# Seven block products instead of eight in 16 of the 22 column pairs of a feed-forward product

## The chip, the cores and the metric

The kernel runs on one core of a Trainium2 chip. The metric is the device time of one execution in microseconds (us). Every time below is of the kernel before the change.

## The reference

One inference step of a small backbone: two trunk layers over 640 tokens (512 latent tokens and 128 context tokens, which share all weights). Each layer is a token mixer of three kinds and then a gated feed-forward block. Everything is fp32, and what the change touches is the feed-forward block:

```python
D_MODEL = 1024
D_FF = -(-8 * D_MODEL // (3 * 256)) * 256      # 2816 = 22 blocks of 128

h = rmsnorm(x, p['g_pre_ffn']) * (1.0 + sc2) + sh2
ff_a, ff_b = jnp.split(h @ p['w_ffn_in'], 2, axis=-1)      # (640,1024) @ (1024,5632)
x = x + gt2 * rmsnorm((jax.nn.silu(ff_a) * ff_b) @ p['w_ffn_out'], p['g_post_ffn'])
```

`sh2`, `sc2`, `gt2` come from a product of the conditioning vector with `w_ada`, one such product in each layer.

## The kernel before

**Layout.** Activations lie feature-major: 128 features in the partitions, tokens along the free axis. The 640 tokens are two halves of 320 (`HALVES`); half 0 holds latent tokens only, half 1 has 192 latent and 128 context tokens, so its modulation is done in two segments (`SEGS`, 192 and 128 wide).

**Products.** TensorE multiplies fp32 data rounded to a shorter format (fp32r). To keep fp32's precision each operand is split into a high and a low part, and one product is three matmuls of a 128x128 weight tile against 320 tokens: `wh`·`h_hi`, `wh`·`h_lo`, `wl`·`h_hi`. `weights` loads four weight tiles in one 256 KB DMA on SyncE's queue (L474; `raw`, [128,512] fp32), and `split` has ScalarE round them to `wh` (L464) and VectorE subtract for `wl` (L465). The rings hold three `raw` and two each of `wh` and `wl`. `gemm_acc` issues the matmuls (L488, nearly all of the kernel's); `gemm` runs over the reduction, 8 tiles of 128 in the first feed-forward product and 22 in the second.

**The feed-forward block.** `w_ffi` has 44 column blocks of 128, in 22 pairs; in pair n the even block is a, the odd one b, and `silu_mul` makes silu(a)·b (silu on ScalarE at L360, the product on VectorE at L1179) and splits it into `fs[n]`, the operand of the second product (`w_ffo`). Pairs 0 to 5 (`NSP` = 6) run first on half 0 alone, while the other half of the layer before it is still being normalised; then on half 1 alone; then pairs 6 to 21 on both halves. One pair on both halves is 2 blocks x 8 reduction tiles x 3 matmuls x 2 halves = 96 matmuls.

**The way into it.** For each half, `w_out`'s product, a norm and a residual add (`post_norm`) give x, which is stored to HBM (`x_store`, L410). `norm_mod` then makes the operand `h` feature tile by feature tile: `stat_end` (the norm's scale), L440 (VectorE, x times scale into a small tile `u`), L445 (ScalarE, adds the shift and rounds to `h` high), L446 (VectorE, `h` low). Half 1's `norm_mod` runs while TensorE works on half 0.

**Filler.** In layer 0 the `w_ada` product of layer 1 is spread over the feed-forward pairs (`fill`, `NFILL`, `NPACE`; matmuls at L272): eight units of one 256 KB DMA and one matmul behind a pair from pair 8 on, through a ring of `AD1` = 7 blocks of two units.

**Order.** A tile scheduler sets each engine's order of work from the program's order, the buffers' rings and the priorities (`WPRI` puts weights early). On an engine instructions run in that order. At the kernel's start SyncE's queue loads the first weights, constants, x (`xT`) and `w_ada` of layer 0 one behind the other.

## Time and profile before

| | us |
|---|---|
| median of 3 runs | 2059.05 |
| lowest and highest | 2057.67, 2059.5 |
| the profiled execution | 2058.47 |
| its span, first to last instruction | 2056.7 |
| TensorE busy in the span | 1992.5 (97%) |
| VectorE busy | 1105.4 (54%) |
| ScalarE busy | 897.3 (44%) |
| HBM traffic over the span | 108 GB/s |
| mean granted TensorE clock | 0.997 of 2.4 GHz |

Engines in the profile: PE is TensorE's matmuls, PEld its weight loads (they overlap PE), DVE is VectorE, ACT is ScalarE, POOL is GpSimd, SP is SyncE, and a q behind an engine's name is its DMA queue. L488 is line 488 of the kernel. A row of a group gives busy time, mean duration in ns, and the idle time just before the group with what ended it. A matmul's duration includes its way through the array, so that the sum over a group exceeds what it occupies; the pace of matmuls is read from their starts, or from a stretch without idle time.

### The profile page before, as it was taken

How to read it: one execution, taken by the hardware profiler on the slowest of the kernel's cores; microseconds unless marked ns; L12 is line 12 of the kernel's file. 1: busy time of each engine (PE TensorE's matmuls, PEld its weight loads, DVE VectorE, ACT ScalarE, POOL GpSimd, SP SyncE). 2: the span in 40 equal slices, each digit the busy share in tenths (PEclk: the TensorE clock that was granted, in tenths of full speed). 3: DMA queues.
4: the chain of work that ended last, by engine and by line, in shares of the span. 5: the costliest groups of instructions: out<-in, count | busy, mean ns of one | idle time of the engine just before them, and what ended most of it. 6: DMA issues, size and time to landing. Idle time of an engine off the chain costs nothing.

```text
span 2056.7 us, 40047 instructions
## 1 busy us (share of the span) xinstructions
PE 1992.5 (97%) x16080; PEld 1777.1 (86%) x16080; DVE 1105.4 (54%) x2570; ACT 897.3 (44%) x1912; POOL 16.4 (1%) x64
## 2 busy tenths in 40 slices
PE   6999999999999999999999999999999999999996
PEld 2748788788999999999987588888899999999996
DVE  5536666785684323222675475778658633322245
ACT  4424254844664222222564352566457533223243
POOL 0000000000000000000000000000000000000000
PEclk9999999999999999999999999999999999999998
DMA  8552211200674332233575431111046432222345
GB/s 293 201 169 66 55 37 50 64 4 28 215 256 134 107 100 77 74 102 85 165 251 197 136 92 45 43 46 41 4 129 211 145 97 73 77 74 83 91 133 159
DMA packets 157995, 226.57 MB, mean 110 GB/s; under 512 B 39280, under 2 KB 66032, under 8 KB 157808
## 3 DMA queue, kind: packets, MB, share of 16 engines
q1 hardware_dynamic: 157168, 222.70, 34.6%
q8 instruction: 126, 2.06, 0.4%
q0 software_dynamic: 640, 1.31, 0.3%
q14 instruction: 61, 0.50, 0.1%
HBM read 209.99 MB, written 12.65 MB: 108 GB/s over the span
## 4 chain that ended last, share of the span: by engine, by line
PE 66%; DVE 6%; ACT 4%; DMA 3%; issue 1%; ACTq 0%; DVEq 0%
PE g L488 53%; PE m L272 2%; DVE wl L465 1%; PE m L817 1%; PE m L1150 1%; ACT wh L464 1%; PE m L872 1%; DMA raw<-in_w_ffi_dram 1%; PE g L1057 1%; DMA raw<-in_w_out_dram 1%; ACT h L353 1%; DMA raw<-in_w_in_dram 1%; DVE smax L1113 1%; DMA raw<-in_w_ffo_dram 0%; PE m L786 0%
## 5 line engine op out<-in xcount | busy, mean ns | idle before, releaser
L488 PE MATMUL g<-h,wh 128*128 128x320 f32 x4496 | 925.0, 314 | 7.0 <-ACT wh L464 3.0
L488 PEld LDWEIGHTS g<-h,wh 128*128 128x128 f32 x4496 | 717.9, 188 | 62.6 <-issue 31.5
L464 ACT ACTIVATE wh<-raw 128x512 fp32r<-128x512 f32 (+2 forms) x538 | 330.9, 616 | 821.1 <-PE g L488 730.5
L465 DVE TENSOR_TENSOR wl<-raw,wh 128x512 fp32r<-128x512 f32 (+2 forms) x514 | 343.9, 670 | 564.6 <-ACT wh L464 547.8
L488 PE MATMUL g<-h,wl 128*128 128x320 f32 x2248 | 572.0, 314 | 1.7 <-DVE wl L465 1.5
L488 PEld LDWEIGHTS g<-h,wl 128*128 128x128 f32 x2248 | 386.8, 188 | 25.4 <-issue 12.7
L488 PE MATMUL g<-w,wh 128*128 128x320 f32 x1152 | 241.9, 310 | 2.4 <-DVE w L465 0.9
L488 PEld LDWEIGHTS g<-w,wh 128*128 128x128 f32 x1152 | 187.9, 188 | 4.9 <-ACT wh L464 1.7
L488 PE MATMUL g<-r,wh 128*128 128x320 f32 x768 | 162.8, 310 | 0.0
L488 PE MATMUL g<-w,wl 128*128 128x320 f32 x480 | 132.2, 314 | 2.7 <-DVE wl L465 1.3
L488 PEld LDWEIGHTS g<-r,wh 128*128 128x128 f32 x768 | 125.9, 188 | 0.7 <-ACT wh L464 0.2
L488 PEld LDWEIGHTS g<-w,wl 128*128 128x128 f32 x480 | 85.5, 188 | 8.1 <-DVE wl L465 8.1
L1179 DVE TENSOR_TENSOR su<-su,g 128x320 f32<-128x320 f32 x88 | 39.9, 484 | 82.2 <-PE g L488 82.2
L488 PE MATMUL g<-r,wl 128*128 128x320 f32 x288 | 79.1, 311 | 0.2 <-DVE wl L465 0.2
L272 PE MATMUL m<-w,silu_c 128*32 128x512 f32 x256 | 77.8, 603 | 0.6 <-DMA w<-in_w_ada_dram 0.6
L353 ACT ACTIVATE h<-m,smax 128x128 f32<-128x128 f32 (+1 forms) x72 | 36.2, 506 | 42.3 <-DVE smax L1116 36.9
L488 PEld LDWEIGHTS g<-r,wl 128*128 128x128 f32 x288 | 51.4, 188 | 0.7 <-DVE wl L465 0.4
L817 PE MATMUL m<-w,w 64*64 64x64 f32 x960 | 46.6, 222 | 0.0
L817 PEld LDWEIGHTS m<-w,w 64*64 64x64 f32 x960 | 42.8, 134 | 2.5 <-issue 2.5
L1150 PE MATMUL m<-h,r 128*128 128x128 f32 x320 | 42.5, 278 | 0.9 <-DVE h L1140 0.9
L572 DVE SCALAR_TENSOR_TENSOR w<-w,vec,w 128x642 f32<-128x642 f32 x48 | 42.5, 885 | 1.2
L872 PE MATMUL m<-w,w 64*64 64x64 f32 x960 | 41.0, 226 | 1.4 <-DVE smax L1123 0.6
(336 smaller groups left out, 2318.8 us busy)
## 6 DMA issues: line engine op xcount, KB each, us to landing
raw<-in_w_ffi_dram SPq DMA_DIRECT2D x224, 256.0 KB, 2.6
w<-in_w_ada_dram SPq DMA_DIRECT2D x160, 256.0 KB, 5.3
raw<-in_w_ffo_dram SPq DMA_DIRECT2D x120, 256.0 KB, 2.7
raw<-in_w_in_dram SPq DMA_DIRECT2D x106, 256.0 KB, 2.9
raw<-in_w_out_dram SPq DMA_DIRECT2D x64, 256.0 KB, 2.7
r<-in_w_ada_dram SPq DMA_DIRECT2D x32, 256.0 KB, 4.0
r<-in_xT_dram SPq DMA_DIRECT2D x6, 640.0 KB, 5.3
xd<-w SPq DMA_DIRECT2D x6, 640.0 KB, 3.8
```

Source lines behind the costliest of these rows:

```text
L272: nc.tensor.matmul(acc[32 * j:32 * j + 32, :], lhsT=self.sc[:, k, :], rhs=raw, start=(k == 0), stop=(k == KD - 1), tile_position=(0, 32 * j))
L353: i = self.nc.scalar.activation(dst, src, f, **kw)
L464: self.nc.scalar.activation(hi, src, AF.Copy)
L465: self.nc.vector.tensor_tensor(out=lo, in0=src, in1=hi.bitcast(F32), op=ALU.subtract)
L488: self.nc.tensor.matmul(ps[h], lhsT=w[:, k], rhs=rhs(e, kk, h), start=(kk == 0 and i == 0), stop=(kk == nk - 1 and i == 2))
L572: nc.vector.scalar_tensor_tensor(out=acc, in0=cb[:, i:i + NT + 2], scalar=w(i), in1=acc, op0=ALU.mult, op1=ALU.add)
L817: nc.tensor.matmul(o, lhsT=a, rhs=b, start=(i == 0), stop=(i == len(ts) - 1))
L872: nc.tensor.matmul(o, lhsT=lhs(c, h), rhs=r, start=True, stop=True)
L1057: nc.tensor.matmul(ps, lhsT=x_, rhs=w[k], start=(k == 0 and i == 0), stop=(k == 1 and i == 2))
L1113: nc.vector.tensor_reduce(out=st[:, j:j + 1], in_=ps, axis=AX.X, op=ALU.max)
L1150: nc.tensor.matmul(ot[:, qt * 128:qt * 128 + 128], lhsT=V[kt // 2][:, kt % 2, vs], rhs=PT[:, kt * 128:kt * 128 + 128], start=(kt == 0), st ...
L1179: nc.vector.tensor_tensor(out=u, in0=u, in1=pb[h], op=ALU.mult)
```

## The change

Take a pair of blocks, the two halves of the reduction (features 0 to 511 and 512 to 1023) and the two halves of the tokens: a 2x2 block product, eight block products of 4 weight tiles x 3 = 12 matmuls each, 96 in all. Winograd's form of Strassen's scheme needs seven, and more additions. `seven` does that for pairs 6 to 21:

- the four weight blocks are loaded raw as before, VectorE makes four sums of them (L507, [128,512]), and seven weight operands are split instead of four (L582 on ScalarE, L583 on VectorE);
- the activation side is needed in seven forms, made once in a layer: `norm_quads` writes `h` in place over x and splits it four feature tiles at a time ([128,1280], `quad`), and `combine` makes four sums of blocks (L478) and splits them too, in the program after pair 0 of half 1;
- the seven results add up in three PSUM tiles (X, Z, Wp), with three copies out by ScalarE (L525, L531, L539) and three VectorE operations that read PSUM (L544, L551, L558); then two silu and two products (L552, L565) as before. The seventh product (`last`) runs inside the next pair, behind its second product;
- silu(a)·b of these pairs is kept as fp32 (`us`) and split into `fs` after the loop, 640 wide.

The raw ring grows from 3 to 7, `wh` and `wl` from 2 to 3, and `AD1` falls from 7 to 3 blocks to make room. The software DMA's scratch on GpSimd is set to 4096 bytes. Pairs 0 to 5 stay as they are, and so do the matmuls' shapes.

```diff
-NRAW = 3
+NRAW = 7
+NSPLIT = 3
 WK = 4
+SCRATCH = 4096
+EPRI = 40000
 WPRI = 20000
...
-AD0, AD1 = 7, 7
+AD0, AD1 = 7, 3
+UTAGS = ("w1", "w1", "w1", "h", "h", "r", "r", "r")
...
+    def norm_quads(self, ts, st, G, sh, half, tag, own):
+        nc = self.nc
+        rs = self.stat_end(st, tag)
+        h0 = HALVES[half][0]
+        parts = []
+        for g in range(2):
+            for i in range(4):
+                k = 4 * g + i
+                for (a, b, s) in SEGS[half]:
+                    v = ts[g][:, i, a - h0:b - h0]
+                    nc.vector.scalar_tensor_tensor(out=v, in0=v, scalar=G[:, k, s:s + 1], in1=rs[:, a - h0:b - h0],
+                                                   op0=ALU.mult, op1=ALU.mult)
+                    nc.scalar.activation(v, v, AF.Identity, bias=sh[:, k, s:s + 1])
+            parts.append(self.quad(ts[g], "h"))
+        return parts
+
+    def quad(self, src, btag):
+        hi, lo = self.blk([128, 4, HALF], F32R, btag), self.blk([128, 4, HALF], F32R, btag)
+        self.split(hi, lo, src)
+        return hi, lo
+
+    def combine(self, t0, t1, tags):
+        nc = self.nc
+        (a11, a12), (a21, a22) = t0, t1
+        op = lambda o, a, b, f=ALU.subtract: nc.vector.tensor_tensor(out=o, in0=a, in1=b, op=f)
+        op(a22, a21, a22)
+        n1 = self.quad(a22, tags[0])
+        op(a21, a11, a21)
+        op(a11, a22, a11)
+        n2 = self.quad(a11, tags[1])
+        n3 = self.quad(a21, tags[2])
+        op(a12, a12, a11, ALU.add)
+        return n1, n2, n3, self.quad(a12, tags[3])
+
+    def seven(self, l, n, A, u, prev, tmp):
...
+        def product(ps, a, w, first):
+            i = 0
+            for e, f in ((0, 0), (0, 1), (1, 0)):
+                for k in range(4):
+                    nc.tensor.matmul(ps, lhsT=w[e][:, k], rhs=a[f][:, k], start=first and i == 0, stop=i == 11,
+                                     skip_group_check=not first)
+                    i += 1
...
+        X, Z, Wp = ps("g0"), ps("g1"), ps("c1")
+        with weight():
+            w11 = operand(b0)
+        product(X, A11, w11, True)
+        with first():
+            nc.scalar.activation(tmp[:, 0], X, AF.Copy)
+        with weight():
+            add(b0, b0, b1)
+            t1 = operand(b0)
+        product(Z, n1, t1, True)
+        with first():
+            nc.scalar.activation(tmp[:, 2], Z, AF.Copy)
+        if prev is not None:
+            prev()
+        with weight():
+            add(b0, b0, b2)
+            t2 = operand(b0)
+        product(X, n2, t2, False)
+        with first():
+            nc.scalar.activation(tmp[:, 1], X, AF.Copy)
+        with weight():
+            w21 = operand(b3)
+        product(Wp, A12, w21, True)
+        with first():
+            nc.vector.tensor_tensor(out=tmp[:, 0], in0=tmp[:, 0], in1=Wp, op=ALU.add)
+        self.silu(tmp[:, 0], tmp[:, 0], False)
+        with weight():
+            w22 = operand(b2)
+            add(b1, b1, b2)
+        product(Z, s4, w22, False)
+        with first():
+            nc.vector.tensor_tensor(out=tmp[:, 1], in0=Z, in1=tmp[:, 1], op=ALU.subtract)
+        nc.vector.tensor_tensor(out=u[:, 0:HALF], in0=tmp[:, 0], in1=tmp[:, 1], op=ALU.mult)
+        with weight():
+            t3 = operand(b1)
+            add(b0, b0, b3)
+        product(X, n3, t3, False)
+        with first():
+            nc.vector.tensor_tensor(out=tmp[:, 2], in0=tmp[:, 2], in1=X, op=ALU.subtract)
+
+        def last():
+            with weight():
+                t4 = operand(b0)
+            product(X, A22, t4, False)
+            self.silu(tmp[:, 3], X, False)
+            nc.vector.tensor_tensor(out=u[:, HALF:NT], in0=tmp[:, 3], in1=tmp[:, 2], op=ALU.mult)
+        return last
...
-            h2[s] = self.norm_mod(x, sx, m["G2"], m["sh2"], s, tag)
-        fs = [self.blk([128, 2, NT], F32R, tag) for tag in ["w0"] * 7 + ["w1"] * 7 + ["r"] * 8]
...
+            h2[s] = self.norm_quads(ts, sx, m["G2"], m["sh2"], s, tag, bt)
+        fs = [self.blk([128, 2, NT], F32R, "w0") for n in range(NSP)]
...
+        A = (h2[0][0], h2[0][1], h2[1][1]) + combos
+        last, us = None, []
+        for i, n in enumerate(range(NSP, NFF)):
+            if i % 2 == 0:
+                pair = self.blk([128, 2, NT], tag=UTAGS[i // 2])
+            us.append(pair[:, i % 2])
+            last = self.seven(l, n, A, us[-1], last, rb([128, 4, HALF]))
+            if n >= NFILL:
+                fill(NPACE)
+        last()
```

The change gives every engine another order of work. TensorE in the loop over pairs 6 to 21 of layer 0, before: `g_1104` and `g_1105` are a block's PSUM tiles of the two halves, and each weight tile meets both halves in turn.

```order
L488 MATMUL g_1104_7297<-h_826_5879,wh_1107_7300 128x320
L488 MATMUL g_1105_7298<-h_890_6267,wh_1107_7300 128x320
L488 MATMUL g_1104_7297<-h_828_5881,wh_1107_7300 128x320
L488 MATMUL g_1105_7298<-h_892_6269,wh_1107_7300 128x320
L488 MATMUL g_1104_7297<-h_826_5879,wl_1108_7301 128x320
L488 MATMUL g_1105_7298<-h_890_6267,wl_1108_7301 128x320
```

The same place after, at the end of pair 8 (the product of `t3`) and the first products of pair 9, with the `w_ada` filler (L276, ring blocks `r_1146` to `r_1148`) and, in the last row, `last` of pair 8:

```order
L513 MATMUL g_1129_7538<-w1_1001_6865,wh_1144_7649 128x320 x4
L513 MATMUL g_1129_7538<-w1_1002_6866,wh_1144_7649 128x320 x4
L513 MATMUL g_1129_7538<-w1_1001_6865,wl_1145_7650 128x320 x4
L276 MATMUL m_1150_7671<-r_1146_7667,silu_c_96 32x512 x2
L276 MATMUL m_1150_7671<-r_1147_7668,silu_c_96 32x512 x2
L276 MATMUL m_1150_7671<-r_1148_7669,silu_c_96 32x512 x2
L513 MATMUL g_1156_7697<-h_826_5887,wh_1159_7700 128x320 x4
L513 MATMUL g_1156_7697<-h_827_5888,wh_1159_7700 128x320 x4
L513 MATMUL g_1156_7697<-h_826_5887,wl_1160_7701 128x320 x4
L276 MATMUL m_1150_7671<-r_1146_7667,silu_c_96 32x512
L513 MATMUL g_1157_7698<-w1_997_6855,wh_1161_7718 128x320 x4
...
L513 MATMUL g_1129_7538<-h_884_6291,wh_1163_7735 128x320 x4
```

A weight operand now serves 12 matmuls in a row on one half, not 24 on both, and a third ring block is reused one product after it was read.

VectorE while TensorE runs half 0's pairs and half 1's `h` is made, before (`u`, `h_890` high and `h_892` low are single feature tiles):

```order
L440 SCALAR_TENSOR_TENSOR u_895_6278<-r_885_6213,G2_116_956,r_887_6217 128x192
L446 SCALAR_TENSOR_TENSOR h_892_6269<-u_894_6271,mods_110_803,h_890_6267 128x192
L446 SCALAR_TENSOR_TENSOR h_892_6269<-u_894_6271,mods_110_803,h_890_6267 128x128
L440 SCALAR_TENSOR_TENSOR u_895_6278<-r_885_6213,G2_116_956,r_887_6217 128x128
L465 TENSOR_TENSOR wl_982_6644<-raw_980_6642,wh_981_6643 128x512
```

After (`h_882` and `h_883` are the first four feature tiles' high and low part, `h_884` and `h_885` those of the last four; `wl_985` is the first low weight of half 1):

```order
L464 SCALAR_TENSOR_TENSOR r_878_6202<-r_878_6202,G2_116_956,r_879_6205 128x128
L583 TENSOR_TENSOR h_883_6272<-r_877_6201,h_882_6271 128x1280
L583 TENSOR_TENSOR wl_973_6717<-raw_971_6715,wh_972_6716 128x512
L583 TENSOR_TENSOR wl_977_6736<-raw_975_6734,wh_976_6735 128x512
L1297 TENSOR_TENSOR su_966_6691<-su_966_6691,g_959_6654 128x320
L583 TENSOR_TENSOR wl_980_6754<-raw_978_6752,wh_979_6753 128x512
L583 TENSOR_TENSOR w0_890_6299<-su_966_6691,w0_890_6299 128x320
L583 TENSOR_TENSOR h_885_6292<-r_878_6202,h_884_6291 128x1280
L583 TENSOR_TENSOR wl_985_6778<-raw_983_6776,wh_984_6777 128x512
L583 TENSOR_TENSOR wl_988_6796<-raw_986_6794,wh_987_6795 128x512
L478 TENSOR_TENSOR r_878_6202<-r_877_6201,r_878_6202 128x1280
L583 TENSOR_TENSOR wl_992_6815<-raw_990_6813,wh_991_6814 128x512
```

Half 1's operand is complete only with two wide splits, the second directly ahead of the first low weights of half 1, and the sums of `combine` stand between the weights behind them.

SyncE's queue at the kernel's start, before:

```order
L474 DMA raw_44_361<-in_w_in_dram 128x512
L474 DMA raw_47_391<-in_w_in_dram 128x512
L474 DMA raw_50_421<-in_w_in_dram 128x512
L206 DMA ct_1_73<-in_cT_dram 128x16
L208 DMA cst_75<-in_cst_dram 128x128
L210 DMA vec_77<-in_vecs_dram 128x250
L474 DMA raw_53_451<-in_w_in_dram 128x512
L474 DMA raw_73_559<-in_w_in_dram 128x512
L239 DMA lbe_3_99<-in_lb_dram 128x4
L404 DMA r_7_118<-in_xT_dram 128x4x320
```

After, behind four `raw` loads that are not repeated here:

```order
L592 DMA raw_73_559<-in_w_in_dram 128x512
L592 DMA raw_76_589<-in_w_in_dram 128x512
L592 DMA raw_83_636<-in_w_in_dram 128x512
L592 DMA raw_86_666<-in_w_in_dram 128x512
L592 DMA raw_93_713<-in_w_in_dram 128x512
L592 DMA raw_96_743<-in_w_in_dram 128x512
L210 DMA ct_1_73<-in_cT_dram 128x16
L212 DMA cst_75<-in_cst_dram 128x128
L214 DMA vec_77<-in_vecs_dram 128x250
L243 DMA lbe_3_99<-in_lb_dram 128x4
L408 DMA r_7_118<-in_xT_dram 128x4x320
```

Ten weight loads instead of three stand ahead of the constants, and ten instead of five ahead of x and `w_ada`.

## Rows read from the trace of the kernel before

**Rows 1.** The page: busy time of each engine; the chain that ended last.

```profile
PE 1992.5 (97%) x16080; PEld 1777.1 (86%) x16080; DVE 1105.4 (54%) x2570; ACT 897.3 (44%) x1912; POOL 16.4 (1%) x64
...
PE 66%; DVE 6%; ACT 4%; DMA 3%; issue 1%; ACTq 0%; DVEq 0%
PE g L488 53%; PE m L272 2%; DVE wl L465 1%; PE m L817 1%; PE m L1150 1%; ACT wh L464 1%; PE m L872 1%; DMA raw<-in_w_ffi_dram 1%; PE g L1057 1%; DMA raw<-in_w_out_dram 1%; ACT h L353 1%; DMA raw<-in_w_in_dram 1%; DVE smax L1113 1%; DMA raw<-in_w_ffo_dram 0%; PE m L786 0%
```

**Rows 2.** PE's waits: what for, us in total, times, longest us.

```profile
PE m L391 <- DVE w L387: 20.4, 4, 17.6
PE g L488 <- ACT wh L464: 3.6, 6, 1.3
PE g L488 <- DVE h L465: 3.0, 1, 3.0
PE g L488 <- DVE wl L465: 2.9, 14, 0.5
```

**Rows 3.** Busy time of each engine in stretches of the span.

```profile
core 0: us, PE busy (x) PEld busy (x) DVE busy (x) ACT busy (x) POOL busy (x), PEclk, DMA share, GB/s
0.00:35.00 35.00, 15.77 (x57) 5.12 (x57) 20.28 (x62) 15.31 (x34) 0.37 (x7) 1.00 0.93 328
...
565.00:654.00 89.00, 88.45 (x576) 83.56 (x576) 62.60 (x134) 53.88 (x104) 0.00 (x0) 1.00 0.64 209
654.00:885.00 231.00, 231.00 (x1582) 224.95 (x1581) 70.08 (x133) 66.50 (x130) 0.00 (x0) 1.00 0.28 89
...
1655.00:1880.00 225.00, 225.00 (x1536) 225.00 (x1535) 69.08 (x126) 65.58 (x129) 0.00 (x0) 1.00 0.25 77
```

**Rows 4.** Timeline of PE near the end of layer 1's pairs: start, duration, instruction.

```profile
1867.70 0.75 PE L488 MATMUL g<-h,wh 128*128 128x320 f32 x4
...
1879.14 0.75 PE L488 MATMUL g<-h,wh 128*128 128x320 f32 x4
```

**Rows 5.** Groups by line and form on DVE and ACT.

```profile
L465 DVE TENSOR_TENSOR wl<-raw,wh 128x512 fp32r<-128x512 f32 x470 | 323.9, 690 | 524.4 <-ACT wh L464 507.7 <-PE g L488 5.5 <-PE m L281 4.0
...
L1179 DVE TENSOR_TENSOR su<-su,g 128x320 f32<-128x320 f32 x88 | 39.9, 484 | 82.2 <-PE g L488 82.2
...
L464 ACT ACTIVATE wh<-raw 128x512 fp32r<-128x512 f32 x494 | 311.5, 631 | 770.8 <-PE g L488 685.3 <-issue 25.1 <-DMA raw<-in_w_ffi_dram 16.6
L360 ACT ACTIVATE su<-g 128x320 f32<-128x320 f32 x88 | 34.1, 424 | 0.0
L464 ACT ACTIVATE w<-su 128x320 fp32r<-128x320 f32 x56 | 25.2, 471 | 2.1 <-DVE su L1179 1.1
...
L353 ACT ACTIVATE w<-w 128x1280 f32<-128x1280 f32 x8 | 10.2, 1273 | 0.8 <-DVE w L847 0.8
```

**Rows 6.** Timeline of SyncE's DMA queue, first 36 us.

```profile
0.76 1.34 SPq L474 DMA_DIRECT2D raw<-in_w_in_dram  x3
...
5.01 0.99 SPq L474 DMA_DIRECT2D raw<-in_w_in_dram  x2
...
9.11 25.51 SPq L303 DMA_DIRECT2D w<-in_w_ada_dram  x32
```

**Rows 7.** Timeline of PE: first matmuls of half 0's pairs, layers 0 and 1.

```profile
564.54 0.56 PE L488 MATMUL g<-h,wh 128*128 128x320 f32 x2 [0.46 <-ACT wh L464]
...
1565.72 0.46 PE L488 MATMUL g<-h,wh 128*128 128x320 f32 x2
```

**Rows 8.** Timeline of ACT and DVE: half 1's `h`, layer 0 and layer 1.

```profile
594.17 0.75 ACT L445 ACTIVATE h<-u,mods 128x192 fp32r<-128x192 f32 x2 [0.55 <-DVE u L440]
...
612.94 0.34 DVE L446 SCALAR_TENSOR_TENSOR h<-u,mods,h 128x128 fp32r<-128x128 f32 x1
...
1597.00 1.08 ACT L445 ACTIVATE h<-u,mods 128x192 fp32r<-128x192 f32 x3
```

**Rows 9.** The page, DMA issues: count, KB each, median us to landing.

```profile
raw<-in_w_ffi_dram SPq DMA_DIRECT2D x224, 256.0 KB, 2.6
...
r<-in_w_ada_dram SPq DMA_DIRECT2D x32, 256.0 KB, 4.0
```

More of the change, by code (lines that the diff above doesn't have):

```diff
@@ new lines, in seven, with operand, add @@
+    def seven(self, l, n, A, u, prev, tmp):
+        nc = self.nc
+        W = self.I["w_ffi"]
+        A11, A12, A22, n1, n2, n3, s4 = A
+        with self.tc.high_priority(offset=WPRI):
+            raw = []
+            for j, g in ((0, 0), (1, 0), (1, 1), (0, 1)):
+                r = self.wp.tile([128, WK * 128], F32, tag="raw", name=self.nm("raw"), bufs=NRAW)
+                nc.sync.dma_start(out=r.rearrange("p (k n) -> p k n", n=128), in_=W[l, 2 * n + j][:, 4 * g:4 * g + 4])
+                raw.append(r)
+        b0, b1, b2, b3 = raw
+        def operand(r):
+            wh = self.wp.tile([128, WK, 128], F32R, tag="wh", name=self.nm("wh"), bufs=NSPLIT)
+            wl = self.wp.tile([128, WK, 128], F32R, tag="wl", name=self.nm("wl"), bufs=NSPLIT)
+            self.split(wh, wl, r.rearrange("p (k n) -> p k n", n=128))
+            return wh, wl
+        def add(o, a, b):
+            nc.vector.tensor_tensor(out=o, in0=a, in1=b, op=ALU.add)
+        def product(ps, a, w, first):
[5 more added lines that the diff above has]
+                    i += 1
+        ps = lambda t: self.pp.tile([128, HALF], F32, tag=t, name=self.nm("g"), bufs=2)
+        first = lambda: self.tc.high_priority(offset=EPRI)
+        weight = lambda: self.tc.high_priority(offset=WPRI)
+        X, Z, Wp = ps("g0"), ps("g1"), ps("c1")
[44 more added lines that the diff above has]
+        return last
@@ L470, in weights @@
             raw = self.wp.tile([128, WK * 128], F32, tag="raw", name=self.nm("raw"), bufs=NRAW)
-            wh = self.wp.tile([128, WK, 128], F32R, tag="wh", name=self.nm("wh"), bufs=2)
-            wl = keep if keep is not None else self.wp.tile([128, WK, 128], F32R, tag="wl", name=self.nm("wl"), bufs=2)
+            wh = self.wp.tile([128, WK, 128], F32R, tag="wh", name=self.nm("wh"), bufs=NSPLIT)
+            wl = keep if keep is not None else self.wp.tile([128, WK, 128], F32R, tag="wl", name=self.nm("wl"), bufs=NSPLIT)
             r3 = raw.rearrange("p (k n) -> p k n", n=128)
@@ L1292, in layer @@
             self.x_store(self.xd[2 * l], s, ts)
-            h2[s] = self.norm_mod(x, sx, m["G2"], m["sh2"], s, tag)
-        fs = [self.blk([128, 2, NT], F32R, tag) for tag in ["w0"] * 7 + ["w1"] * 7 + ["r"] * 8]
-        ffi = lambda n, halves: self.gemm(I["w_ffi"][l, n], lambda e, k, s: h2[s][e](k), KD, halves)
+            xs[s] = ts
+            h2[s] = self.norm_quads(ts, sx, m["G2"], m["sh2"], s, tag, bt)
+        fs = [self.blk([128, 2, NT], F32R, "w0") for n in range(NSP)]
+        ffi = lambda n, halves: self.gemm(I["w_ffi"][l, n], lambda e, k, s: h2[s][k // 4][e][:, k % 4], KD, halves)
         filler = self.ada(l + 1, tuple(g for g in range(3) if g not in GR[l + 1]), "c0", "r", AD1) if l + 1 < L else iter(())
-        for halves, ns in (((0,), range(NSP)), ((1,), range(NSP)), ((0, 1), range(NSP, NFF))):
-            for n in ns:
+        for halves in ((0,), (1,)):
+            for n in range(NSP):
                 pa = ffi(2 * n, halves)
                 pb = ffi(2 * n + 1, halves)
-                with self.tc.high_priority(offset=SPRI if n < NSP and 0 in halves else 0):
+                with self.tc.high_priority(offset=SPRI if 0 in halves else 0):
                     self.silu_mul(fs[n], pa, pb)
-                if n >= NFILL:
-                    fill(NPACE)
+                if n == 0 and 1 in halves:
+                    combos = self.combine(xs[0], xs[1], ("w1", "r", "w1", "r"))
+        A = (h2[0][0], h2[0][1], h2[1][1]) + combos
[8 more added lines that the diff above has]
+        last()
         fill(100)
         self.retable()
+        for u, tag in zip(us, ["w0"] * (7 - NSP) + ["r"] * 4 + ["w1"] * 7 + ["r"] * 4):
+            fs.append(self.blk([128, 2, NT], F32R, tag))
+            self.split(fs[-1][:, 0], fs[-1][:, 1], u)
         ys = [self.wide("r") for s in range(2)]
@@ L1434 @@
     from concourse.bass_utils import run_bass_kernel_spmd as _run
-    nc = _bacc.Bacc("TRN2", target_bir_lowering=False, num_devices=1)
+    nc = _bacc.Bacc("TRN2", target_bir_lowering=False, num_devices=1, dynamic_dma_scratch_size=SCRATCH)
     arrays, I, O = {}, {}, {}
```

## The prediction

> **What bounds the kernel now.** I read the page's busy line first: PE is busy 97% of the span, DVE 54%, ACT 44%, and most of the chain that ended last is PE, over half of the span on the one matmul line L488 [rows 1]. Then PE's waits: apart from the start (17.6 us on the first norm's squares) none adds up to more than 4 us, and those that a weight split ends come to 3.6 and 2.9 us [rows 2]. Then the windows: in the stretch of both halves' pairs PE has no idle time at all, 225.00 us of 225.00 in layer 1 and 231.00 of 231.00 in layer 0; DVE is busy 69 of the 225 us and the DMA queues a quarter; the granted clock is 1.00, the upper of the two levels, 2.4 GHz [rows 3]. So the stage that is changed is bound by the number of matmuls, and the question is whether DVE, ACT and the loads keep up with fewer.
>
> **The term that saves.** Layer 1's window holds 1536 matmuls of 320 columns in 225.00 us, 146.5 ns each [rows 3]. The timeline says the same: from 1867.70 to 1879.14 lie 13 groups of six, 11.44 us or 146.7 ns each [rows 4]. The three steps of a pair, reuse of a weight on two halves or not, don't matter: every matmul has its own weight load already. Removed are 96 - 84 = 12 matmuls in each of 16 pairs in 2 layers, 384. 384 x 0.1465 = **-56.3 us**. A pair takes 12.3 us instead of 14.1.
> By the Trainium skill ("TensorE: Matmul & The Clock Gate", Back-to-back issue gap) warm matmuls start N/2.4 + 2.5 ns apart, for 320 columns 135.8 ns as an estimate from that page; the saving would be 52.1 us. The trace's 146.5 ns differs, and the measurement decides.
>
> **What is added in the loop, per pair.** DVE: seven low splits and four sums of [128,512] at 690 ns and five operations of [128,320] at 484 ns, 7.6 + 2.4 = 10.0 us of the 12.3 (81%; before, 69 us in 16 pairs, 4.3 of 14.1). The sums have no row; I take the split's, the same operation on the same shape. ACT: seven high splits at 631 ns, three copies at 471, two silu at 424, 6.7 us [rows 5]. SyncE loads the same four blocks. Both engines fit beside PE, product by product too: a product is 12 x 0.1465 = 1.76 us, and an operand with its sum costs DVE 1.38. The products that also meet PSUM operations need up to 2 x 0.69 + 2 x 0.484 = 2.35 us; the 0.6 us excess has to come from the lead of the three-deep split rings (up to two products, 3.5 us). Walking DVE's order with these durations, each split and each PSUM operation ends at least 1 us before its product starts. I count 0, with 0.5 us for each pair (16 us in all) as the upper bound.
>
> **Entry into half 1, each layer.** Before, half 1's `h` comes tile by tile, the last low part at 612.94, while PE is already in half 1 [rows 8]; that was cover that the change removes. Now nothing of it can be used before a four-tile split ends. Layer 0: half 0 starts at 564.54 [rows 7] and has 288 matmuls, 42.2 us, plus about 0.8 for the statistics' matmuls between them: PE is due in half 1 at 607.5. ACT's first shift comes at 594.17 [rows 8]. Up to `h_884` ACT has 16 shifts (three in 1.08 us, 0.36 each; 5.8 us [rows 8]), six weight splits (0.63, some 0.53 back to back; 3.2), a silu and two 320-wide splits (about 1.0), and two 1280-wide splits (1.27 each by the nearest row, an exponential of that width [rows 5]; 2.5): 12.5 us, end 606.7, plus some 0.8 for shifts that wait for DVE. DVE then makes `h_885`, 128x1280, which has no row: from 484 at 320 and 690 at 512 the slope is 1.07 ns a column, 1.5 us as an estimate [rows 5]. Directly behind it in DVE's queue stands `wl_985`, which half 1's third matmul needs: 607.5 + 1.5 + 0.7 = 609.7, against 607.8 due, a stall of 1.9 us. In layer 1 the shifts start at 1597.00, half 0 at 1565.72 [rows 7, 8]: 1.6 us nearer to the end, stall 3.5. Behind it `combine` puts four sums and four low splits of 1.5 us between low weights that are due every 1.76 us; 1.5 + 0.7 = 2.2 runs late by 0.4 eight times, 3.5 us, less what the ring of three holds ahead: 1 us a layer. Sum **+7.4**; bounds 0 (the scheduler's lead suffices) and 14 (no lead).
>
> **Filler.** Layer 0's window has 46 matmuls more than layer 1's and takes 6.0 us more, 0.13 each [rows 3]. With three ring blocks a burst of six reads them all; the seventh needs the first block again, whose load can be issued once the burst's first two matmuls have read it, and PE comes to it four filler matmuls (0.5) and one product (1.76) later, 2.3 us. A load of that size lands 2.6 us after its issue, those into this tag in the median 4.0 [rows 9]. With 0.4 for the issue PE waits 0.7 to 2.1, in each of the four filled pairs of layer 0: **+4** (taken 1.0 each, nearer to the short landing, since the queues are only a quarter busy here [rows 3]); bounds 0 and 8. While SyncE stands at such a load the raw loads behind it wait as well; the ring of seven holds more than a pair's four, which covers that.
>
> **Start.** Ten raw loads instead of five precede x and `w_ada`. Five issues at 1.34/3 = 0.45 us are 2.2 us; five times 262 KB at the 328 GB/s of this stretch, in which the queues are 93% busy, 4.0 [rows 3, 6]. PE's first work waits for x (17.6 us, [rows 2]), and everything up to 35 us follows the loads. **+3**; bounds 0 and 4.
>
> **Deeper rings elsewhere.** PE's waits for high and low weights are 6.5 us in all [rows 2]; that is the most that rings can give back. Against it, every stage gets a new order, which can cost as much. **-3**; bounds -6.5 and +4.
>
> **At nothing.** The `us` splits (16 of 640 columns, 0.83 us on DVE as an estimate by the slope above) replace 320-wide ones that were on DVE too. The second product takes a reduction tile each 0.88 us (six matmuls); four such splits and a weight split cost DVE 4.0 us where PE takes 3.5. The six tiles split earlier are 5.3 us of lead, of which 16 tiles use up 2: `w_ffo`'s first matmuls hide them; without that lead it is 2 us a layer. The in-place norm must wait for `x_store`, whose transfer has landed before the norm's scale is ready. The smaller GpSimd scratch concerns 8 transfers off PE's path.
>
> **Sum.** -56.3 + 0 + 7.4 + 4 + 3 - 3 = -44.9. Against the profiled execution, 2058.47, that is 2013.6; the median of the runs lies 0.6 above it, so I forecast **2014 us**, 2.2% faster.
>
> **Rivals.**
> *All hidden (chance 0.15).* The entry, the filler and the start cost their lower bounds, and rings give 3 to 6: 2059.1 - 56.3 less 3 to 6.5, about **1998** (1996 to 2003). For it: the waits that PE has in the trace of before are short everywhere behind the start [rows 2]. Against it: the walk above, in which `wl_985` stands behind a wide split in a queue that runs in order.
> *The loop stalls a little (chance 0.20).* Each pair loses about 0.7 us, one operation of DVE that PE is kept waiting for, 32 x 0.7 = 22 us on top of the forecast: **2036** (2026 to 2054). For it: DVE at 81% with five operations a pair that wait for a product's end; against it: the ring's lead.
> *Slower: DVE's queue becomes the bound of the loop (chance 0.03).* A PSUM operation at the head of DVE's queue waits for the last of 12 matmuls; the next product's low split stands behind it. Each time the split ring has no lead left, PE waits 0.484 + 0.69 = 1.2 us. The point from which it decides is 1.76 us a pair, what a pair saves, so one and a half such meetings. With two of the five a pair, 2.4 us, the loop alone costs 32 x (2.4 - 1.76) = +20 us, with the other terms **2091**. For it: no low split is made in the trace of before with such a share of DVE. Against it: the order puts each such operation one product or more behind the one that it reads.
> The Trainium skill says of the queues ("TensorE: Matmul & The Clock Gate", Architectural detail: the array is 16x 32x32, not 1x 128x128) that ACT and DVE run strictly first in, first out; no run here shows otherwise. Could a waiting operation be passed in the queue, this rival's 0.03 would go to the forecast.
> *No change (chance 0.02)*: a mixture of these with the sum near 0, 2055 to 2063.
>
> **How the numbers follow.** The forecast's own case has 0.60; with its terms half way to their bounds at once (entry 3.7 to 10.7, filler 2 to 6, start 1.5 to 3.5, rings -4.7 to 0.5) it spans 2005 to 2024. The other two that end faster have 0.15 and 0.20. I give 1998 to 2034 as the range: 0.60, about half of "all hidden" and about half of "a little". A measurement here can tell 0.2% (4 us) from no change, so faster is all that ends below 2055: 0.60 + 0.15 + 0.20 = 0.95; same 0.02; slower 0.03.
>
> **What would show it.** Right: L513 and the first product's matmuls together number 384 fewer; the windows of pairs 6 to 21 are 197 us plus stalls instead of 225, with PE busy throughout and DVE at about 80%. Entry: a PE wait for DVE `wl` or `h` L583 of 2 to 4 us in each layer at the start of half 1. Filler: four waits of L276 for the load of `r`, each 0.5 to 2. Start: PE's first matmul at 20 to 22 us instead of 17.6. Wrong: PE's idle time in the loop ended by L583, L507 or the ACT copies in every pair (rivals two and three), or matmuls of the loop at another pace than 146.5 ns, which would upset the first term and with it the forecast.

## The result, and the profile after

The changed kernel takes 2005.61 us (median of 4 runs, 2005.08 to 2006.44) against 2059.28 for the kernel before beside it: ratio 0.9741, 95% interval 0.9724 to 0.9758, 53.7 us less. The forecast was 2014, its range 1998 to 2034. The profiled execution took 2005.87, its span is 2004.1.

The page's busy time of each engine (compare [rows 1]); the matmuls now stand on two lines, L606 (`gemm_acc`) and L513 (`seven`):

```profile
PE 1938.8 (97%) x15696; PEld 1724.3 (86%) x15696; DVE 1296.2 (65%) x2834; ACT 1001.2 (50%) x2088; POOL 16.4 (1%) x64
```

384 matmuls fewer, 16080 to 15696, and PE is busy 53.7 us less; DVE rose from 1105 to 1296 us, ACT from 897 to 1001. PE's waits (what for, us in total, times, longest; compare [rows 2]):

```profile
PE m L395 <- DVE w L391: 22.7, 3, 21.0
PE g L606 <- ACT r L1405: 5.5, 2, 2.8
...
PE m L276 <- DMA r<-in_w_ada_dram: 0.5, 2, 0.3
PE g L606 <- DVE wl L583: 0.5, 2, 0.2
```

The start waits 3.3 us longer. A new wait stands second: PE waits twice for L1405, ScalarE's copy of `w_out`'s result out of PSUM. The filler's loads (L276) and the weight splits hardly appear. The stretches of `w_out` before layer 0's feed-forward block, of pairs 6 to 21 in layer 0 and in layer 1, and of the second product of layer 1 (columns as in [rows 3]):

```profile
506.39:567.30 60.91, 57.95 (x389) 56.87 (x388) 37.76 (x69) 42.09 (x86) 0.00 (x0) 1.00 0.62 194
...
655.16:871.89 216.73, 216.23 (x1420) 201.06 (x1418) 152.81 (x270) 108.94 (x207) 0.00 (x0) 1.00 0.38 118
...
1635.18:1833.15 197.97, 197.97 (x1352) 197.86 (x1351) 151.71 (x264) 107.99 (x206) 0.00 (x0) 1.00 0.29 87
1833.15:1989.83 156.68, 155.10 (x1056) 154.42 (x1054) 64.45 (x110) 57.65 (x110) 0.00 (x0) 1.00 0.43 124
```

The same pairs and the same second product in the kernel before, between the same events:

```profile
655.94:889.06 233.12, 233.12 (x1596) 227.07 (x1595) 70.08 (x133) 66.59 (x131) 0.00 (x0) 1.00 0.28 89
...
1654.74:1880.03 225.29, 225.29 (x1539) 225.29 (x1538) 69.14 (x126) 65.81 (x129) 0.00 (x0) 1.00 0.25 77
1880.03:2042.43 162.40, 159.12 (x1061) 155.20 (x1059) 60.71 (x105) 55.83 (x107) 0.00 (x0) 1.00 0.43 125
```

Layer 1's pairs are what the scheme promises: 197.97 us, of which 8 matmuls (1.2 us) are the second product's, so 196.8 against 225.3, 28.5 less, without idle time on PE and with DVE busy 77%. Layer 0's pairs give only 17.6 by the same reckoning (216.7 less 1.2, against 233.1), and the second product, which the scheme doesn't touch, gives 5.7 (4.5 without those 8). So the sum came out near, but from other terms. In us, between events that all kernels share, with two of the experiments below beside them (the rings alone in the kernel before; the changed kernel with two edits):

| stretch | before | rings alone | after | after, two edits |
|---|---|---|---|---|
| to the first `w_in` matmul | 32.9 | 36.8 | 36.3 | 34.6 |
| mixer 0 | 471.2 | 470.8 | 470.1 | 470.2 |
| `w_out` 0 | 60.4 | 57.9 | 60.9 | 57.9 |
| pairs 0 to 5 on each half, layer 0 | 91.4 | 86.9 | 87.9 | 88.7 |
| pairs 6 to 21, layer 0 | 233.1 | 234.0 | 216.7 | 211.6 |
| `w_ffo` 0 and mixer 1 | 615.6 | 611.0 | 613.2 | 611.5 |
| `w_out` 1 | 61.0 | 58.0 | 62.2 | 57.9 |
| pairs 0 to 5 on each half, layer 1 | 89.0 | 86.9 | 87.9 | 88.7 |
| pairs 6 to 21, layer 1 | 225.3 | 225.3 | 198.0 | 198.0 |
| `w_ffo` 1, to the last norm | 162.4 | 157.4 | 156.7 | 156.7 |
| rest | 14.3 | 14.3 | 14.3 | 14.3 |

### The profile page after: what moved, and what is told of

It reads as the page before. It is cut to its first block, busy times and chain, and to the rows that moved or that the text cites. A ratio compares the mean times of both kernels' runs of the same rounds, so it can differ in the third digit from the quotient of the medians.

```text
span 2004.1 us, 39984 instructions
## 1 busy us (share of the span) xinstructions
PE 1938.8 (97%) x15696; PEld 1724.3 (86%) x15696; DVE 1296.2 (65%) x2834; ACT 1001.2 (50%) x2088; POOL 16.4 (1%) x64
## 5 line engine op out<-in xcount | busy, mean ns | idle before, releaser
L582 ACT ACTIVATE wh<-raw 128x512 fp32r<-128x512 f32 (+2 forms) x634 | 391.4, 617 | 591.9 <-PE g L606 410.1
L583 DVE TENSOR_TENSOR wl<-raw,wh 128x512 fp32r<-128x512 f32 (+1 forms) x610 | 408.8, 672 | 376.0 <-ACT wh L582 336.0
L606 PE MATMUL g<-h,wh 128*128 128x320 f32 x2448 | 541.3, 318 | 1.6 <-DVE su L1297 0.7
L606 PEld LDWEIGHTS g<-h,wh 128*128 128x128 f32 x2448 | 397.4, 188 | 50.2 <-issue 28.8
L606 PE MATMUL g<-h,wl 128*128 128x320 f32 x1224 | 337.1, 316 | 0.5 <-DVE wl L583 0.5
L606 PE MATMUL g<-w,wh 128*128 128x320 f32 x1152 | 242.5, 311 | 5.5 <-ACT r L1405 5.5
L606 PEld LDWEIGHTS g<-h,wl 128*128 128x128 f32 x1224 | 215.9, 188 | 21.4 <-issue 15.6
L606 PEld LDWEIGHTS g<-w,wh 128*128 128x128 f32 x1152 | 188.8, 189 | 6.3 <-ACT r L1405 6.0
L606 PE MATMUL g<-r,wh 128*128 128x320 f32 x768 | 162.9, 310 | 0.0
L606 PE MATMUL g<-w,wl 128*128 128x320 f32 x480 | 131.0, 310 | 0.0
L513 PE MATMUL g<-h,wh 128*128 128x320 f32 x768 | 129.1, 310 | 0.0
L606 PEld LDWEIGHTS g<-r,wh 128*128 128x128 f32 x768 | 125.9, 188 | 0.5
L513 PEld LDWEIGHTS g<-h,wh 128*128 128x128 f32 x768 | 116.3, 188 | 3.6 <-issue 3.4
L507 DVE TENSOR_TENSOR raw<-raw,raw 128x512 f32<-128x512 f32 x128 | 88.0, 688 | 2.2
L606 PEld LDWEIGHTS g<-w,wl 128*128 128x128 f32 x480 | 86.0, 189 | 0.2
L513 PE MATMUL g<-w,wh 128*128 128x320 f32 x512 | 85.9, 310 | 0.0
L513 PE MATMUL g<-r,wh 128*128 128x320 f32 x512 | 85.5, 309 | 0.0
L276 PE MATMUL m<-w,silu_c 128*32 128x512 f32 x256 | 83.4, 603 | 0.2 <-DMA w<-in_w_ada_dram 0.2
L513 PEld LDWEIGHTS g<-w,wh 128*128 128x128 f32 x512 | 77.6, 188 | 3.4 <-ACT r L525 3.4
L606 PE MATMUL g<-r,wl 128*128 128x320 f32 x288 | 78.6, 309 | 0.0
L513 PEld LDWEIGHTS g<-r,wh 128*128 128x128 f32 x512 | 77.7, 188 | 0.0
L513 PE MATMUL g<-h,wl 128*128 128x320 f32 x384 | 71.9, 309 | 0.0
```

The source lines that it names most:

```text
L276: nc.tensor.matmul(acc[32 * j:32 * j + 32, :], lhsT=self.sc[:, k, :], rhs=raw, start=(k == 0), stop=(k == KD - 1), tile_position=(0, 32 * j))
L507: nc.vector.tensor_tensor(out=o, in0=a, in1=b, op=ALU.add)
L513: nc.tensor.matmul(ps, lhsT=w[e][:, k], rhs=a[f][:, k], start=first and i == 0, stop=i == 11, skip_group_check=not first)
L582: self.nc.scalar.activation(hi, src, AF.Copy)
L583: self.nc.vector.tensor_tensor(out=lo, in0=src, in1=hi.bitcast(F32), op=ALU.subtract)
L606: self.nc.tensor.matmul(ps[h], lhsT=w[:, k], rhs=rhs(e, kk, h), start=(kk == 0 and i == 0), stop=(kk == nk - 1 and i == 2))
```

## The experiments

**The rings alone.** My theory had them at a small sum of opposite terms.

```diff
 # the kernel before
-NRAW = 3
+NRAW = 7
...
-            wh = self.wp.tile([128, WK, 128], F32R, tag="wh", name=self.nm("wh"), bufs=2)
-            wl = keep if keep is not None else self.wp.tile([128, WK, 128], F32R, tag="wl", name=self.nm("wl"), bufs=2)
+            wh = self.wp.tile([128, WK, 128], F32R, tag="wh", name=self.nm("wh"), bufs=3)
+            wl = keep if keep is not None else self.wp.tile([128, WK, 128], F32R, tag="wl", name=self.nm("wl"), bufs=3)
...
-    nc = _bacc.Bacc("TRN2", target_bir_lowering=False, num_devices=1)
+    nc = _bacc.Bacc("TRN2", target_bir_lowering=False, num_devices=1, dynamic_dma_scratch_size=4096)
```

> The kernel before with the deeper rings alone (raw 3 to 7, high and low weights 2 to 3, the smaller GpSimd scratch that makes room); all 44 column blocks still by eight products. Theory: the change's time comes from the 384 matmuls alone (-56), and the rings by themselves are a small sum of opposite terms: +3.3 at the start (PE's first matmul at about 20.9 us instead of 17.6), about +5 in layer 1's mixer, where the order breaks up the w_ada filler, and -8 to -12 where a weight tile serves one half only (half stages, the last column blocks of w_ffo, w_in at half 0), so 2054 to 2060. Rival A, the rings hardly matter but for the start: 2062 to 2063. Rival B, a good part of the gain is the rings': below 2045.

Measured: 2040.82 us, ratio 0.9911 (0.9897 to 0.9926), 17.6 less, though the start is 3.9 later. That is rival B, and my theory falls: without the start the rings give 21.5. My bound, PE's visible waits for weights (6.5 us), was no bound. How PE's waits escape the list is seen in the timeline of the kernel before, where the second product changes to a new weight tile in a stretch on one half (start, duration, instruction):

```profile
1997.37 0.31 PE L488 MATMUL g<-r,wl 128*128 128x320 f32 x1
1997.51 0.46 PE L488 MATMUL g<-w,wh 128*128 128x320 f32 x2
1998.09 0.42 PE L488 MATMUL g<-w,wl 128*128 128x320 f32 x1
```

and at the same change of tile with the rings:

```profile
1983.59 0.31 PE L488 MATMUL g<-r,wl 128*128 128x320 f32 x1
1983.74 0.46 PE L488 MATMUL g<-w,wh 128*128 128x320 f32 x2
1984.03 0.31 PE L488 MATMUL g<-w,wl 128*128 128x320 f32 x1
```

From the first of two matmuls on the new `wh` to the first on `wl` it takes 0.29 us with the rings (1983.74 to 1984.03) and 0.58 before (1997.51 to 1998.09), so PE is 0.29 late. The row at 1998.09 has no idle time beside it: at the usual pace a matmul's shown end lies some 0.17 us behind the start of the next, so that much of the 0.29 is covered, and the 0.12 that is left isn't printed. The Trainium skill (Perfetto Trace Analysis, Tensor Engine Instruction) says that the profiler estimates a matmul's end from its size and doesn't observe it; these rows agree, since the two matmuls on `wh` are shown to last 0.46 us in both kernels, with the pause behind them and without. In before's last 162 us such late starts add up to about 5.5 us (some 26 places), of which the rows show 0.9 as idle; with the rings it is 0.2 us at one place. The count of matmuls would have said it: 1056 x 0.1467 = 154.9 us of work in 162.4.

**Which of the rings.** The first run has the edit of the splits (and of the scratch) without that of `NRAW`, the second that of `NRAW` (and of the scratch) without that of the splits:

```diff
-NRAW = 3
+NRAW = 7
```

> The kernel before with only the rings of high and low weights at three (raw stays at three; smaller GpSimd scratch). The full deeper rings took 18 us off the kernel before, far more than PE's visible waits for weights (6.5). Reading starts of matmuls instead of idle time, about 20 us of small gaps of 0.1 to 0.3 us ahead of matmuls on a new weight tile are in the trace of before where a tile serves one half only, and 4 with the deeper rings. Theory: those gaps come from the ring of two splits (a split can't begin before the tile two back has been used up), so this edit alone gives nearly all, and the start stays as before (PE's first matmul at 17.6): 2036 to 2041. Rival: they come from the raw ring (the next load is issued too late), then 2052 to 2059.

> The kernel before with only the raw ring at seven (splits stay at two; smaller GpSimd scratch). Theory that the gaps belong to the split rings: no gain, and the later start costs 3 to 4, 2060 to 2064. Rival, they belong to the raw ring: 2040 to 2045.

Measured: 2046.34 for the splits (0.9942, 0.9925 to 0.9958), 2048.06 for raw (0.9943, 0.9929 to 0.9958): 12 us each. Neither expectation holds; each alone gives some two thirds of the whole. In the last stretch the splits alone give nearly all (157.8 us, against 157.4 with both, 160.2 with raw at seven and 162.4 before); from the second product of layer 0 through mixer 1 both give much the same, 3.8 and 3.3 us. What divides the rest was not separated.

**Eight products again.**

```diff
             product(X, A22, t4, False)
+            product(X, A22, t4, False)
```

> The changed kernel with the seventh product of each pair issued twice, so that a pair is 96 matmuls again with all of the new additions, splits and orders (that one product is counted twice in the sums, which changes what is computed). Theory, the loop is bound by the number of matmuls and nothing else: 32 x 12 x 0.1467 = +56.3, 2061 to 2063, and layer 1's loop 225 us as before the change. Rival, DVE or ACT already set a part of the loop's time: the extra product is partly covered, below 2055.

Measured: 2061.72, 56.1 more than the changed kernel, and layer 1's pairs:

```profile
1661.76:1888.28 226.52, 226.52 (x1547) 226.46 (x1546) 155.64 (x270) 109.69 (x208) 0.00 (x0) 1.00 0.25 77
```

225.3 us without the second product's 8 matmuls, what it was before. The theory holds: the saving is the number of matmuls, 384 x 0.1465, in full, and none of it hides behind DVE or ACT. It also shows what all the rest of the change costs together: 2061.72 against 2059.59 for the kernel before beside it, 2 us, where the forecast's other terms came to 11.4.

**How far DVE is from being the bound.** The condition is `< 3` in the first run (three of a pair's seven operands) and `< 7` in the second (all seven).

```diff
-            self.split(wh, wl, r.rearrange("p (k n) -> p k n", n=128))
+            r3 = r.rearrange("p (k n) -> p k n", n=128)
+            self.split(wh, wl, r3)
+            self.nop = (getattr(self, 'nop', -1) + 1) % 7
+            if self.nop < 3:
+                nc.vector.tensor_tensor(out=wl, in0=r3, in1=wh.bitcast(F32), op=ALU.subtract)
```

> The changed kernel with three of the seven low splits of each pair done twice on DVE (the same values again), 0.69 us each. DVE's busy time in layer 1's loop goes from 152 to about 185 of 198 us (94%). Theory, DVE has 2.8 us a pair to spare and its lead through the rings of three evens out the rest: 2005 to 2009. Rival, DVE's queue, in order and waiting for PSUM, is at its limit at 77%: each extra operation is paid, up to 32 x 2.07 = 66 us, and anything above 2020 speaks for it.

> The changed kernel with all seven low splits of each pair done twice on DVE (4.8 us a pair more; with three, 2.07 us, nothing moved). DVE's work is then 9.5 + 4.8 = 14.3 us a pair, over PE's 12.3. Theory, DVE becomes the bound only when its work exceeds PE's: the pairs take 14.3 us, +2.0 x 32 = 64, 2066 to 2076, so about what the change before would have had to add on DVE to lose its gain. Rival, an in-order queue waiting for PSUM loses more than its sum: above 2085. Other rival, still covered: below 2040.

Measured: 2008.12 with three (ratio 0.9751, 0.9736 to 0.9765), 2052.43 with seven (0.9964, 0.9952 to 0.9977). Layer 1's pairs, with three and then with seven:

```profile
1635.03:1833.00 197.97, 197.91 (x1348) 197.39 (x1347) 177.76 (x310) 106.78 (x206) 0.00 (x0) 1.00 0.29 87
```

```profile
1651.13:1877.93 226.80, 210.81 (x1353) 198.12 (x1352) 212.47 (x371) 104.52 (x207) 0.00 (x0) 1.00 0.24 74
```

At 90% DVE costs PE nothing, the stretch is the same to a hundredth. With seven, DVE is busy 94% of 226.8 us, and PE waits, by its list over the whole run, for ScalarE's high splits. In layer 1's pairs these wait for DVE in turn, for its low splits (L507) and its sums (L511), and DVE waits for them:

```profile
PE g L517 <- ACT wh L586: 23.5, 27, 1.0
...
ACT wh L586 <- DVE wl L507: 10.3, 14, 0.7
ACT wh L586 <- DVE raw L511: 7.7, 5, 4.0
...
DVE wl L587 <- ACT wh L586: 12.6, 27, 0.8
```

So DVE can become the loop's bound, more than three operations per pair away. What does it here isn't the slower rival's mechanism: the last row is all that DVE's list of waits has in this stretch, none for a result in PSUM. The run came out cheaper than I expected (2066 to 2076, with 32 us for each layer). Layer 1's pairs are 28.8 us longer than in the changed kernel, layer 0's only 17.9:

```profile
653.97:888.57 234.60, 224.72 (x1420) 201.08 (x1419) 212.46 (x377) 105.77 (x208) 0.00 (x0) 1.00 0.35 107
```

Most of the miss is layer 0's. There PE has the filler to do as well, and DVE's work probably goes on beside it; that was not tested by itself. The smaller part is that I summed durations of 0.69 us, but DVE's [128,512] operations start 0.61 us apart when they stand back to back.

**The copies of `w_out`.** In the changed kernel ScalarE's queue before PE's wait is (start, duration):

```profile
554.61 1.26 ACT L582 ACTIVATE h<-w 128x1280 fp32r<-128x1280 f32 x1
555.77 0.62 ACT L582 ACTIVATE wh<-raw 128x512 fp32r<-128x512 f32 x1
556.29 1.46 ACT L466 ACTIVATE w<-w,mods 128x320 f32<-128x320 f32 x3
557.65 0.62 ACT L582 ACTIVATE wh<-raw 128x512 fp32r<-128x512 f32 x1
558.17 1.26 ACT L582 ACTIVATE h<-w 128x1280 fp32r<-128x1280 f32 x1
559.33 0.46 ACT L389 ACTIVATE r<-r 128x320 f32<-128x320 f32 x1
559.69 0.74 ACT L1405 ACTIVATE r<-g 128x320 f32<-128x320 f32 x2
```

and PE meanwhile:

```profile
557.09 0.31 PE L606 MATMUL g<-r,h 128*128 128x320 f32 x1
560.16 0.56 PE L606 MATMUL g<-w,wh 128*128 128x320 f32 x2 [2.76 <-ACT r L1405]
```

Half 0's wide splits and shifts stand ahead of two copies, and with two PSUM tiles PE can't go on.

```diff
-                nc.scalar.activation(y(n), ps[s], AF.Copy)
+                with self.tc.high_priority(offset=EPRI):
+                    nc.scalar.activation(y(n), ps[s], AF.Copy)
```

> The changed kernel with one edit: ScalarE's copies of w_out's result out of PSUM get the priority that the loop's copies have. Theory: the two waits of 2.76 us, in which PE stood for a PSUM tile while ScalarE worked through half 0's shifts and two 1280-wide splits, go; half 0's first matmul in layer 0 comes at about 564.5 instead of 567.3: 2000 to 2001. Rival, the work is only moved on ScalarE and half 0's operand or its weights come later by the same time: 2005 to 2006, with the wait ended by h or wh at half 0's first matmul instead.

Measured: 1998.35 (0.9711, 0.9694 to 0.9727), 7.3 less by the medians, 6.2 by the ratios. Both `w_out` stretches are 57.9 us, and the wait has left the list. The theory holds, with a little more than its 2000 to 2001; a small wait for ScalarE's silu takes its place (1.8 us), and pairs 0 to 5 take 0.8 us more in each layer.

In the traces the two stretches give 7.4 us, more than the 5.5 of waits, and 1.3 of it are slower matmuls behind one of the waits. In the changed kernel `w_out` of layer 1 takes 62.23 us, 1.3 more than layer 0's 60.91, at a mean granted clock of 0.97 against 1.00, and its matmuls behind the wait start 0.27 us apart instead of 0.147 for a while, the pace of the lower level of 1.2 GHz:

```profile
1485.08:1547.31 62.23, 59.28 (x388) 58.20 (x388) 37.84 (x69) 42.07 (x86) 0.00 (x0) 0.97 0.60 191
...
1538.84 0.90 PE L606 MATMUL g<-w,wh 128*128 128x320 f32 x2 [2.75 <-ACT r L1405]
1539.54 0.47 PE L606 MATMUL g<-w,wl 128*128 128x320 f32 x1
1539.81 0.73 PE L606 MATMUL g<-w,wh 128*128 128x320 f32 x2
```

In layer 0 the same wait has no such sequel, and in the run with six filler units below both `w_out` stretches have it (0.97, 62.2 us each). With the copies put first both are at 1.00.

**The filler.** First its ring in the kernel before, then its bursts in the changed one.

```diff
 # the kernel before
-AD0, AD1 = 7, 7
+AD0, AD1 = 7, 3
```

> The kernel before with the filler's ring in the feed-forward block at 3 blocks instead of 7, nothing else. Theory: the ring of three breaks the bursts of eight filler units into six and single ones; a single unit takes PE about 0.98 us where one in a burst takes 0.31, so the eight or so new single units cost 5, with a few tenths for waits on their loads: 2063 to 2066, the pairs of layer 0 longer by 5 to 8 us than before (233.1 us from pair 6 to the second product). Rival, the ring's depth costs only what PE visibly waits for the loads, below 1 us: 2059 to 2060.

```diff
 # the changed kernel
-NSP, NFILL, NPACE = 6, 8, 8
+NSP, NFILL, NPACE = 6, 8, 6
```

> The changed kernel with six filler units behind a pair instead of eight, which is what three ring blocks hold, over six pairs instead of four. Theory: the eight single units become two, each 0.98 us against 0.31 in a burst: -4, and the waits for their loads, 0.5, go: 2001 to 2002. Rival, the filler's cost in the loop (18.8 us more in layer 0 than in layer 1) is the units' own work and doesn't depend on how they stand together: 2005 to 2006.

Measured: the ring of three costs the kernel before about 7 us, 2065.71 against 2058.38 (1.0034, 1.0021 to 1.0046; pairs 6 to 21 of layer 0 go from 233.1 to 240.1). Six units a pair give the changed kernel 5.5 back, 2000.08 (0.9715, 0.9700 to 0.9729), a little more than the 4.5 expected. Both theories hold in their main point, and the reason is seen in the changed kernel's PE timeline behind pair 9 (two records a filler unit):

```profile
724.40 1.91 PE L276 MATMUL m<-r,silu_c 128*32 128x512 f32 x12
726.24 1.44 PE L513 MATMUL g<-h,wh 128*128 128x320 f32 x8
727.51 0.75 PE L513 MATMUL g<-h,wl 128*128 128x320 f32 x4
728.47 1.04 PE L276 MATMUL m<-r,silu_c 128*32 128x512 f32 x2 [0.21 <-DMA r<-in_w_ada_dram]
729.44 1.44 PE L513 MATMUL g<-w,wh 128*128 128x320 f32 x8
730.72 0.60 PE L513 MATMUL g<-w,wl 128*128 128x320 f32 x3
731.25 1.04 PE L276 MATMUL m<-r,silu_c 128*32 128x512 f32 x2
732.23 0.41 PE L513 MATMUL g<-w,wl 128*128 128x320 f32 x1
```

against a burst of eight in the kernel before:

```profile
729.66 1.92 PE L272 MATMUL m<-r,silu_c 128*32 128x512 f32 x16
731.52 0.71 PE L488 MATMUL g<-h,wh 128*128 128x320 f32 x3
```

Eight units take 1.86 us together, six take 1.84, and each of the two left over takes 0.97 alone: 3.8 us a pair instead of 1.9, with 0.2 us of visible wait. The units write four groups of 32 columns of the array in turn, and neighbours overlap; a unit alone has no neighbour. So it isn't the number of units in a burst that costs, as the expectations have it (0.31 each), but the number of rounds of up to four: six cost as much as eight, and four together (here from mixer 1 of the changed kernel) as much as one:

```profile
1058.17 1.06 PE L276 MATMUL m<-w,silu_c 128*32 128x512 f32 x8
1059.17 0.42 PE L606 MATMUL g<-h,wh 128*128 128x320 f32 x1
```

Each burst or single unit also costs 0.2 us at its edges: in the rows behind pair 9 the three matmuls ahead of a unit take 0.53 us instead of 0.44 (730.72), and the eight behind the burst 1.27 instead of 1.17 (726.24). Over four pairs that makes 7.8 us for the rounds, 1.6 for the edges, and 0.8 for waits on loads, 10 in all.

**The start.**

```diff
-        self.setup()
-        xs = [self.x_load(self.I["xT"], s, "r")[1] for s in range(2)]
+        with self.tc.high_priority(offset=60000):
+            self.setup()
+            xs = [self.x_load(self.I["xT"], s, "r")[1] for s in range(2)]
...
-        h = self.start(xs, "c0", "w0", 7)
+        with self.tc.high_priority(offset=60000):
+            h = self.start(xs, "c0", "w0", 7)
```

> The changed kernel with the constants, x and layer 0's first w_ada loads put ahead of the raw weights on SyncE's queue at the start. Theory, the ring of seven costs 3.3 us at the start because ten weight loads stand ahead of what PE waits for: PE's first matmul back to 17 us or less, the first of w_in at 32 to 33 instead of 36.3, 2001 to 2003. Rival, the loads of that stretch are the bound, and weights that come later only move the wait: the first w_in matmul stays at 35 to 37 and waits for its weights, 2004 to 2007.

Measured: 2008.46 (0.9748, 0.9733 to 0.9762), no gain: PE starts at 12.0 us and then waits for what now comes last:

```profile
0.00:44.53 44.53, 23.48 (x77) 6.45 (x77) 30.14 (x95) 23.74 (x54) 0.80 (x13) 0.95 0.94 339
...
44.53 0.90 PE L606 MATMUL g<-h,wh 128*128 128x320 f32 x2 [7.38 <-ACT wh L582]
```

The rival's mechanism holds, though not its numbers (35 to 37 us, 2004 to 2007): the DMA queues are 94% busy up to that matmul, and PE waits for what is loaded last. The first `w_in` matmul comes 8.3 us later than in the changed kernel; mixer 0 behind it makes up 5.3 of them. An order with some weights between x and `w_ada` was not tried.

**Together.** The second of these has the edits of the copies and of the filler, the first has the start's as well.

> The changed kernel with all three edits: the priority of w_out's copies (alone -7.3), six filler units a pair (alone -5.5) and the start's loads reordered. Theory, the three places are far apart and add up: -13 and what the start gives (0 to -3), 1989 to 1993. Rival, a new order in one place undoes another's gain: 1994 to 2000.

> The changed kernel with the priority of w_out's copies and six filler units a pair, its own order of loads at the start. Theory, the two gains add up (-7.3 and -5.5), since the run with the start reordered too lost at the start what it gained nowhere: first w_in matmul at about 36 us, 1991 to 1994. Rival, the two gains share something (both change the stretch before the pairs): 1995 to 1999.

Measured: 1995.49 (0.9684, 0.9669 to 0.9698) and 1994.18 (0.9686, 0.9670 to 0.9703). They beat the changed kernel by 10 and 11 us; the start's edit adds nothing. The first expectation missed by 2.5 us: the edit of the start costs some 3 us alone (2008.46), and with these in place of a gain the sum of the three edits is met. The second came out at its upper end. In the table above both gains are there in full, less the 0.8 us twice in pairs 0 to 5.

## Why the prediction was right, term by term

The forecast of 45 us was 9 short of 54, and it was right because its largest term was. That the others partly cancelled was luck: the rings gave 18 us more than I took, the filler, the entry and the stretch behind it cost 11 more.

- *The saving, -56.3.* Right: 28.5 in layer 1's pairs, 56.1 when the product is put back.
- *DVE and ACT fit beside PE, 0.* Right: 77% measured for 81%, no idle time, and room for three more operations a pair. Neither the rival of a loop that stalls nor the slower one showed at 90% DVE; PE lost time to DVE only in the run at 94%.
- *Deeper rings, -3, at most -6.5.* The step that failed: "that is the most that rings can give back" took the list of waits as the whole of PE's lateness. Alone the rings give 21.5 besides the start. The number was there to be read, as matmuls times pace against the length of each stretch on one half.
- *Entry into half 1, +7.4.* Size right by chance, place wrong. The stalls of 1.9 and 3.5 us at half 1's first products didn't come. `h_885` took 1.49 us as estimated, and `wl_985` stood behind it as the order said:

```profile
608.25 0.69 DVE L583 TENSOR_TENSOR wl<-raw,wh 128x512 fp32r<-128x512 f32 x1 [0.68 <-ACT wh L582]
608.86 0.48 DVE L583 TENSOR_TENSOR w<-su,w 128x320 fp32r<-128x320 f32 x1
609.78 1.49 DVE L583 TENSOR_TENSOR h<-r,h 128x1280 fp32r<-128x1280 f32 x1 [0.43 <-ACT h L582]
611.19 1.29 DVE L583 TENSOR_TENSOR wl<-raw,wh 128x512 fp32r<-128x512 f32 x2
...
611.87 0.46 PE L606 MATMUL g<-h,wh 128*128 128x320 f32 x2
612.16 0.31 PE L606 MATMUL g<-h,wl 128*128 128x320 f32 x1
```

  but PE reached half 1 only at 611.87, not 607.5, and its first matmul on `wl_985` (612.16) waits for nothing. Half 0 had begun 2.8 us later, and from its first matmul to half 1's it takes 44.6 us, in this kernel and with the rings alone, not 43.0: the statistics' matmuls between take some 2.4 us, which I had put at 0.8. PE's delay ahead of half 0 was the same burst of shifts and wide splits one half earlier, which my walk had passed over because `h` of half 0 itself was hidden: I asked when the operand is ready, not who stands behind it in ScalarE's queue. Against the rings alone `w_out` is 3.0 and 4.2 us longer (1.3 of the 4.2 at the lower clock), pairs 0 to 5 1.0 each, in two late starts among the first pairs of half 1, where `combine` runs, as the last part of the term had it: 9.2.
- *Filler, +4.* The place right, the mechanism wrong: I priced waits for loads (0.7 to 2.1 each, measured 0.2 to 0.3), while single units cost their overlap. The 0.13 us a matmul was a misreading, too: the window of layer 0 ends at 885, before its pairs do at 889.06, so that it holds fewer of the pairs' matmuls than layer 1's window. Pairs 6 to 21 of layer 0 are 18.8 us longer than layer 1's; with the rings alone 8.7. So 10.
- *Start, +3.* 3.3 in this trace; the other runs with `NRAW` at seven and the old order show 1.6 to 3.9 for the first `w_in` matmul.

Against the rings alone the change is worth 35 us (2040.82 to 2005.61): 56.3 less 10 for the filler, 9 for the entry and 3 between layer 0's second product and mixer 1's end. Some 2 of these 3 lie within the spread between executions: that stretch is 613.2 us in this trace and 611.3 to 613.6 in those of the changed kernel's other runs, whose edits are elsewhere. What the rest is stays open.
